# Attention inside a decoder layer: groups of score products and of value products kept whole in TensorE's order

## The chip, the cores and the metric

The kernel runs on one core of one Trainium2 chip. The metric is the device time of one execution in microseconds; the median of several runs is given. TensorE (PE in the profile, its weight loads PEld) multiplies matrices into PSUM banks; VectorE (DVE), ScalarE (ACT) and GpSimd (POOL) do the element-wise work; SyncE (SP) issues most DMAs.

## The reference

One decoder layer in float32: 2048 tokens, model width 1024. An RMS norm and one input projection give queries, keys and values for an attention with a window of 128 tokens, and the input of a convolution branch; both branches go through one output projection; a SwiGLU network with inner width 2816 follows.

```python
q = proj[..., :512].reshape(B, S, 8, 64)            # 8 query heads
k, v = ...                                          # 2 key/value heads of 64, 4 query heads share one
# blocks of 128 queries; each sees its own block of keys and the one before
s = jnp.einsum("bnqhgd,bnkhd->bnhgqk", qb, kb) * scale
s = jnp.where(in_band & not_before_start, s + bias, -inf)
m = jnp.maximum(max(s), sink)
p = jnp.exp(s - m); p = p / (sum(p) + jnp.exp(sink - m))
o = jnp.einsum("bnhgqk,bnkhd->bnqhgd", p, vb)
conv_out = conformer_conv(u, ...)                   # GLU, causal depthwise conv of width 31, LayerNorm, silu, pointwise
h = h + rms_norm(concat([o, conv_out]) @ w_out, mix_post_g)
h = h + rms_norm((silu(hn @ w_gate) * (hn @ w_up)) @ w_down, ffn_post_g)
```

## The kernel before

The tokens are worked on in four tiles of 512 (t = 0 to 3). Stage A_t makes the input projection of tile t, one output block of 128 columns after the other (`proj(u)`: 24 products of 128x128 by 128x512, since each float32 operand is split in a high and a low half and three products are made of each pair). Stage B_t is the attention of tile t, C_t the convolution branch with its 31 taps on VectorE, U a folding of weights, W_w the output projection, H and F the first half of the feed-forward network, G its second half. The names stand behind the @ in the tiles of the profile (`tr@B`, `mm@A`).

**Generators and lanes.** Each stage is a Python generator that emits instructions and then yields an estimate of TensorE's time. `run` drives the main stages; after each yield it pumps the lanes (`lb` for attention, `lc` for taps, `lw`, `ld`, `lf`, `lh` and others) by that estimate. So attention instructions are emitted between the projections of the next tile: B0 beside A1, B1 beside A2, and so on. Each instruction gets a running number as priority (`tc.cur_priority`; a smaller number goes first; the taps' lane adds 100). At build time a scheduler puts the instructions of each engine in a fixed order, by these numbers and by its own timeline of when operands and buffers will be there. On the chip each engine works its list in that order and waits at semaphores.

**Ties.** `tc.add_manual_dep` with the class `NoSync` only says that one instruction comes after another in the scheduler's order; with `Sync` the instruction also waits on a semaphore for the other to finish.

**Attention of a block of 128 queries.** `front(b)` makes the scores. Head pairs are stacked so that the two key/value heads lie in the two halves of the partitions; a product uses 64 of the 128 rows of the array, and the products of the two halves (g = 1 and 0) go to two PSUM banks. For each `ip` (0 and 1) two query tiles are used: twelve products into two banks, one group. TensorE's `tr` banks are three, shared by scores, transposes and value products. VectorE then masks (`copy_predicated`, L451) and adds the bias while taking the maximum (`tensor_tensor_reduce`, L454). `back(b)` normalizes, transposes the probabilities on TensorE (L491), ACT copies them (L492), POOL cuts them to the window's two triangles (`affine_select`, L494), and the value products follow: four products of 128 rows by 64 columns of the array, into the two halves of one bank, each in float32 and seen as two records in the profile (the first block has half of them). The order of emission is front(0), front(1), back(0), front(2), back(1), front(3), back(2), back(3).

`after_first(first, r)` ties a product behind another with `NoSync`. In a score group all products are tied behind the second, the second behind the first; in a value group all are tied behind the first. Nothing ties a group to another, and nothing holds the first product until the rest can go: in a group the first product is of g = 1, and the second, of g = 0, writes to the other bank.

All products go through the helper `mat` (L85), so in the profile they share that line and are told apart by their tiles: `tr@B<-kz,ql@A` are scores, `tr@B<-p@B,vtok` value products, `mm@...` products that use the whole array.

Of the kernel before, what the change touches and what calls it, by code (L numbers as in the profile page):

```python
# [12 lines left out]
F32 = mybir.dt.float32  # L13
# [5 lines left out]
ALU = mybir.AluOpType  # L19
# [18 lines left out]
def layer_kernel(ctx, tc, x, xT, cols, rows, sinks, relb, onehot, w_in, w_pw, w_out, w_gate, w_up, w_down, out):  # L38
# [22 lines left out]
    def f2(tag, shape=(P, T)):  # L61
        return t_(tag, shape)
# [108 lines left out]
            stt(y, w, d, y, ALU.add, ALU.mult)  # L171
        return y

    def after_first(first, r):
        tc.add_manual_dep(
            r.ins,
            first.ins.name,
            mybir.DependencyInfo(mybir.DependencyClass.NoSync, mybir.DependencyReason.DATA),
            reason="both halves of the array start together",
        )  # L180

    def three(o, pairs, first=True, last=True):
# [59 lines left out]
    y_scr = dr.tile([4, P, S], F32, name="y_scr")  # L242
    hT = [dr.tile([KC, P, T], F32, name=f"hT{i}") for i in range(2)]
    qs = {}
    started = set()

    def load_x(t):
# [74 lines left out]
    def stage_a(t, hn, before_kv, hooks, post=None):  # L322
        L = f"A{t}"
        lab[0] = L
        raw0 = [w0 if t == 0 else None]
        rb = None

        def proj(u):
            w = kweight(u, t > 0, raw0.pop() if raw0 else None)
            o = mm()  # L330
            for k in range(KC):
                three(o, [(w[k], (hn[k][:, 0], hn[k][:, 1]))], k == 0, k == KC - 1)
                for _ in range(FILL[k] if t == u == 0 else 0):
                    mat(warm[:, 0:P], ident, ident, start=True, stop=True)
            return o

        def step(u):
            if u in hooks:
                hooks[u]()
            lab[0] = L  # L340

        def glu(c, og, oa):
            lab[0] = L
            th = f2("fa")
            if post:
                vtt(th, og, rb, ALU.mult)
                act(th, th, AF.Tanh, scale=0.5)
            else:
                act(th, og, AF.Tanh, scale=0.5)
            if oa is None:  # L350
                oa = yield th
            g = f2("fa")
            stt(g, th, 1.0, oa, ALU.add, ALU.mult)
            if post:
                (ptt if 2 * c < TAPS0 else vtt)(g, g, rb, ALU.mult)
            nc.sync.dma_start(glu_scr[c, :, t * T : (t + 1) * T], g)
            started.add(f"g{t}{c}")
            yield

        for c in range(4):  # L360
            og = proj(2 * c)
            if post and c == 0:
                yield 5.2
                step(0)
                late = og, proj(1)
                next(post)
                yield 5.2
                step(1)
                continue
            if post and c == 1:  # L370
                rb = next(post)
                next(glu(0, *late))
            half = glu(c, og, None)
            next(half)
            yield 5.2
            step(2 * c)
            half.send(proj(2 * c + 1))
            yield 5.2
            step(2 * c + 1)
        before_kv()  # L380
        lab[0] = L
        ok = proj(8)
        if t:
            act(kz[:, :, 0:P], kz[:, :, T : T + P].bitcast(F32), AF.Copy)
        if post:
            kt = f2("fa")
            vtt(kt, ok, rb, ALU.mult)
            ok = kt
        act(kz[:, 0, P:], ok, AF.Copy)
        vtt(kz[:, 1, P:], ok, kz[:, 0, P:].bitcast(F32), ALU.subtract)  # L390
        yield 5.2
        step(8)
        ov = proj(9)
        vt = f2("fa")
        if post:
            vtt(vt, ov, rb, ALU.mult)
        else:
            act(vt, ov, AF.Copy)
        yield 5.2
        step(9)  # L400
        q = []
        for i in range(4):
            oq = proj(10 + i)
            if i == 0:
                pv = mm()
                for s in range(4):
                    nc.tensor.transpose(pv[:, s * P : (s + 1) * P], vt[:, s * P : (s + 1) * P], ident)
                if t:
                    nc.vector.tensor_copy(vtok[:, 0], vtok[:, 4])
                nc.vector.tensor_copy(vtok[:, 1:5].rearrange("p a b -> p (a b)"), pv)  # L410
            qi = hl("ql")
            if post:
                qt = f2("fa")
                stt(qt, oq, 0.125, rb, ALU.mult, ALU.mult)
                act(qi[:, 0], qt, AF.Copy)
                vtt(qi[:, 1], qt, qi[:, 0].bitcast(F32), ALU.subtract)
            else:
                act(qi[:, 0], oq, AF.Copy, scale=0.125)
                stt(qi[:, 1], oq, 0.125, qi[:, 0].bitcast(F32), ALU.mult, ALU.subtract)
            q.append(qi)  # L420
            yield 5.2
            step(10 + i)
        qs[t] = q

    def stage_b(t):
# [3 lines left out]
        def front(b):  # L429
            lab[0] = L  # L430
            first = t == 0 and b == 0
            tok = slice(b * P, (b + 1) * P)
            win = slice(b * P, b * P + 256)
            mx = sm(8)
            pr = f4("p", (P, 8, P))
            for ip in range(2):
                os = [tr().rearrange("p (j k) -> p j k", j=2) for _ in range(2)]
                lead = []
                for j in range(2):
                    i = 2 * ip + j  # L440
                    for n, (a, k) in enumerate(((0, 0), (0, 1), (1, 0))):
                        for g in (1, 0):
                            sl = slice(64 * g, 64 * g + 64)
                            r = mat(os[g][:, j], q[i][sl, a, tok], kz[sl, k, win], start=n == 0, stop=n == 2)
                            if lead:
                                after_first(lead[-1], r)
                            if len(lead) < 2:
                                lead.append(r)
                for g in range(2):
                    prev = neg.unsqueeze(2).to_broadcast([P, 2, P]) if first else os[g][:, :, 0:P]  # L450
                    nc.vector.copy_predicated(os[g][:, :, P:], upper.unsqueeze(1).to_broadcast([P, 2, P]), prev)  # L451
                    for j in range(2):
                        h = 4 * g + 2 * ip + j
                        nc.vector.tensor_tensor_reduce(  # L454
                            out=pr[:, h],
                            in0=os[g][:, j, P:],
                            in1=bias[0][:, h],
                            op0=ALU.add,
                            op1=ALU.max,
                            scale=1.0,  # L460
                            scalar=NEG,
                            accum_out=mx[:, h : h + 1],
                        )
                yield 1.3
                lab[0] = L
            negm = sm(8)
            stt(negm, mx, -1.0, nsnk, ALU.mult, ALU.min)
            es = sm(8)
            vtt(es, negm, snk, ALU.add)
            act(es, es, AF.Exp)  # L470
            den = sm(8)
            for h in range(8):
                act(pr[:, h], pr[:, h], AF.Exp, bias=negm[:, h : h + 1], accum_out=den[:, h : h + 1])
            vtt(den, den, es, ALU.add)
            rd = sm(8)
            nc.vector.reciprocal(rd, den)
            live[b] = pr, rd
            yield YC

        def back(b):  # L480
# [3 lines left out]
            for g in range(2):  # L484
# [6 lines left out]
                    nc.tensor.transpose(o[:, i * P : (i + 1) * P], pr[:, 4 * g + i], ident)  # L491
                act(pg[:, 1], o, AF.Copy)  # L492
                for kb in range(1 if first else 0, 2):
                    nc.gpsimd.affine_select(  # L494
                        out=pg[:, kb].rearrange("p (i q) -> p i q", q=P),
                        in_=pg[:, 1].rearrange("p (i q) -> p i q", q=P),
                        compare_op=ALU.is_ge if kb else ALU.is_gt,
                        fill=0.0,
                        base=0,
                        pattern=[[0, 4], [1 if kb else -1, P]],  # L500
                        channel_multiplier=-1 if kb else 1,
                    )
# [3 lines left out]
            lab[0] = L  # L506
            o = tr()
            lead = None
            for kb in (1,) if first else (1, 0):
                for g in (1, 0):  # L510
                    sl = slice(64 * g, 64 * g + 64)
                    r = mat(o[sl], vtok[:, b + kb, sl], pt[g][:, kb], start=kb == 1, stop=first or kb == 0)
                    if lead is None:
                        lead = r
                    else:
                        after_first(lead, r)
            at = f2("at")
            act(at, o, AF.Copy)
            c0 = t * T + b * P
# [3 lines left out]
            yield 1.8  # L523

        live = {}
        for b in range(5):
            if b < 4:
                yield from front(b)
# [820 lines left out]
    RT = 0.2  # L1349
    RP = 0.1  # L1350
    TIE = 5
    AHEAD = 3
    PRES = {0: 20, 2: 16}
    Q0 = 8
# [171 lines left out]
```

## Time and profile before

| what | value |
|---|---|
| median of 3 runs | 1982.09 us (1979.29 to 1984.77) |
| profiled execution | 1987.9 us, its span 1986.2 us |
| mean granted clock of TensorE | 0.987 |
| attention's products on TensorE | 98 to 586 us of the span |
| score products | 384, of 64x256 |
| value records | 124, of 128x512 |

The span runs from the first to the last instruction of the profiled execution; the time is some 1.7 us longer. In the timeline each row gives the start in us, the duration, the engine, the line, the operation, output<-inputs, the shape and a count of like instructions in a row; in brackets stands idle time before it and what ended it. Matmuls are pipelined, so that rows overlap: what one costs is seen from its start to the start of the next. In the table of stretches, PEclk is the granted share of TensorE's clock and DMA the mean busy share of the 16 DMA engines. "issue" as the end of a wait means that the engine waited for nothing that the profile shows.

### The profile page before, as it was taken

What the parts mean: (1) busy time and instruction counts of PE and PEld (TensorE: products, weight loads), DVE (VectorE), ACT (ScalarE), POOL (GpSimd) and SP (SyncE); (2) the same over time, 40 slices, a digit from 0 to 9 for tenths busy, and PEclk for the clock granted to TensorE, in tenths of its full rate; (3) what the DMA queues carried; (4) which work ended last, traced back from release to release, by engine and by line L of the source; (5) the groups of instructions that cost most, each with busy time, mean ns of one, the idle gap of its engine ahead of it and who ended that gap; (6) DMA issues with size and microseconds to landing.
All of it is one profiled execution on the core that took longest, in us unless ns stands there. A gap on an engine that the chain in (4) does not pass through costs nothing.

```text
span 1986.2 us, 26652 instructions
## 1 busy us (share of the span) xinstructions
PE 1930.4 (97%) x8730; PEld 1546.7 (78%) x8730; DVE 1476.3 (74%) x2648; ACT 961.8 (48%) x1886; POOL 304.3 (15%) x427
## 2 busy tenths in 40 slices
PE   8999999999999699999999999999899999999997
PEld 6877777777777588778888878887688888888886
DVE  5999969995874899787759965666866775555557
ACT  5455354447647544334345464656533433345443
POOL 4011011111121101220000110000023332311003
PEclk9999999999999799999999999999899999999999
DMA  8787657566658668775478777759844542375664
GB/s 311 251 303 219 210 187 256 185 212 214 225 195 281 232 218 266 260 266 184 130 253 276 259 255 242 249 202 309 293 140 169 179 140 96 132 244 181 211 195 144
DMA packets 209578, 435.67 MB, mean 219 GB/s; under 512 B 21752, under 2 KB 39328, under 8 KB 209440
## 3 DMA queue, kind: packets, MB, share of 16 engines
q1 hardware_dynamic: 191648, 402.52, 60.7%
q0 software_dynamic: 7040, 23.07, 3.5%
q10 hardware_dynamic: 10752, 8.39, 1.3%
q8 instruction: 68, 1.11, 0.2%
q14 instruction: 70, 0.57, 0.1%
HBM read 323.26 MB, written 110.63 MB: 218 GB/s over the span
## 4 chain that ended last, share of the span: by engine, by line
PE 77%; DVE 8%; DMA 7%; issue 3%; POOL 2%; ACT 2%; SPq 0%; DVEq 0%; POOLq 0%; ACTq 0%
PE mm@F L85 32%; PE mm@G L85 16%; PE mm@A L85 15%; PE mm@W L85 4%; PE tr@B L85 4%; PE tr@W L85 2%; DVE fc@C L94 2%; DMA wx@G<-w_down 1%; DMA gb@F<-keeps 1%; PE mm@U L85 1%; DVE w@F L94 1%; DVE hl@G L94 1%; PE tr@B L491 1%; DMA td<-wx@G 1%; DMA fc@G<-w_down 1%
## 5 line engine op out<-in xcount | busy, mean ns | idle before, releaser
L94 DVE SCALAR_TENSOR_TENSOR fc@C<-glu@C,colt,fc@C 128x512 f32<-128x512 f32 x480 | 357.3, 758 | 2.6
L85 PE MATMUL mm@F<-hl@H,w@F 128*128 128x512 f32 x1056 | 261.3, 397 | 10.2 <-ACT mm@F L939 10.2
L85 PEld LDWEIGHTS mm@F<-hl@H,w@F 128*128 128x128 f32 x1056 | 201.0, 192 | 54.6 <-ACT mm@F L939 12.5
L85 PE MATMUL mm@G<-hl@G,hl@G 128*128 128x512 f32 x924 | 227.7, 393 | 1.1 <-DVE hl@G L94 1.1
L821 ACT ACTIVATE w@F<-chl@F 128x512 fp32r<-128x512 f32 x220 | 135.9, 626 | 187.8 <-PE mm@F L85 149.6
L85 PE MATMUL mm@A<-hl@A,w@A 128*128 128x512 f32 x840 | 209.5, 397 | 4.2 <-ACT w@A L127 1.5
L85 PEld LDWEIGHTS mm@G<-hl@G,hl@G 128*128 128x128 f32 x924 | 171.7, 188 | 37.3 <-DVE hl@G L94 1.9
L85 PE MATMUL mm@G<-w@G,hl@G 128*128 128x512 f32 x876 | 199.4, 389 | 0.0
L85 PEld LDWEIGHTS mm@G<-w@G,hl@G 128*128 128x128 f32 x876 | 164.4, 188 | 34.1
L85 PEld LDWEIGHTS mm@A<-hl@A,w@A 128*128 128x128 f32 x840 | 156.6, 189 | 42.9 <-issue 3.3
L94 DVE TENSOR_TENSOR w@F<-chl@F,w@F 128x512 fp32r<-128x512 f32 x198 | 151.4, 768 | 49.0 <-ACT w@F L821 48.8
L85 PE MATMUL mm@F<-mid@H,w@F 128*128 128x512 f32 x528 | 136.5, 398 | 20.3 <-ACT w@F L821 13.3
L85 PEld LDWEIGHTS mm@F<-mid@H,w@F 128*128 128x128 f32 x528 | 101.0, 192 | 43.7 <-ACT w@F L821 14.1
L85 PE MATMUL mm@F<-ql@H,w@F 128*128 128x512 f32 x528 | 130.0, 392 | 0.0
L85 PE MATMUL mm@F<-p@H,w@F 128*128 128x512 f32 x528 | 129.1, 389 | 0.0
L85 PE MATMUL mm@F<-x@H,w@F 128*128 128x512 f32 x528 | 126.9, 391 | 0.0
L85 PEld LDWEIGHTS mm@F<-ql@H,w@F 128*128 128x128 f32 x528 | 99.1, 189 | 20.8
L85 PEld LDWEIGHTS mm@F<-p@H,w@F 128*128 128x128 f32 x528 | 99.1, 188 | 20.6
L85 PEld LDWEIGHTS mm@F<-x@H,w@F 128*128 128x128 f32 x528 | 98.4, 188 | 21.1 <-issue 0.8
L127 ACT ACTIVATE w@A<-raw@A 128x512 fp32r<-128x512 f32 x110 | 67.5, 626 | 92.1 <-PE mm@A L85 62.1
L94 DVE TENSOR_TENSOR w@G<-raw@G,w@G 128x512 fp32r<-128x512 f32 x73 | 52.1, 713 | 73.0 <-ACT w@G L821 71.8
L494 POOL TENSOR_SCALAR_AFFINE_SELECT p@B<-p@B 128x512 f32<-128x512 f32 x62 | 51.7, 843 | 338.4 <-ACT p@B L492 337.1
(314 smaller groups left out, 3290.1 us busy)
## 6 DMA issues: line engine op xcount, KB each, us to landing
mids<-fa@F SPq DMA_DIRECT2D x154, 256.0 KB, 2.7
raw@A<-w_in SPq DMA_DIRECT2D x55, 512.0 KB, 4.6
w@A<-lo_in SPq DMA_DIRECT2D x84, 256.0 KB, 3.3
fc@G<-mids SPq DMA_DIRECT2D x77, 256.0 KB, 3.4
fa@G<-mids SPq DMA_DIRECT2D x75, 256.0 KB, 4.4
gb@F<-keeps SPq DMA_DIRECT2D x72, 256.0 KB, 3.5
w@W<-fold SPq DMA_DIRECT2D x32, 512.0 KB, 5.9
raw@F<-w_gate SPq DMA_DIRECT2D x22, 512.0 KB, 4.0
```

The costliest lines, as they stand in the source:

```text
L85: r = nc.tensor.matmul(*args, **kw)
L94: r = op(*args, **kw)
L127: act(w[:, 0], raw, AF.Copy)
L491: nc.tensor.transpose(o[:, i * P : (i + 1) * P], pr[:, 4 * g + i], ident)
L494: nc.gpsimd.affine_select(out=pg[:, kb].rearrange("p (i q) -> p i q", q=P), in_=pg[:, 1].rearrange("p (i q) -> p i q", q=P), compare_op=AL ...
L821: act(w[:, 0], x, AF.Copy)
```

## The change

`after_first` gets an argument for the kind of tie. Three things follow in stage B. First, groups get an order among each other: the first product of a score group is tied (order only) behind the last product of the group before it, the first value product behind the last score product, and the next score group behind the last value product (`group[0]`). Second, the first product waits on semaphores: a score group's for the second reduction (g = 0, j = 1) of the score group before it (`scored[0]`), in block 0 also for the low half of its second query tile (`q_ready`); a value group's for the last `affine_select` (`cut`). Third, the products of both kinds are emitted with a priority number that is smaller by 100 (`SOON`).

```diff
-    def after_first(first, r):
+    def after_first(first, r, how="NoSync"):
         tc.add_manual_dep(
             r.ins,
             first.ins.name,
-            mybir.DependencyInfo(mybir.DependencyClass.NoSync, mybir.DependencyReason.DATA),
-            reason="both halves of the array start together",
+            mybir.DependencyInfo(getattr(mybir.DependencyClass, how), mybir.DependencyReason.DATA),
+            reason="products of half the array stand together",
         )
...
+    q_ready = {}
...
-                vtt(qi[:, 1], qt, qi[:, 0].bitcast(F32), ALU.subtract)
+                r = vtt(qi[:, 1], qt, qi[:, 0].bitcast(F32), ALU.subtract)
             else:
                 act(qi[:, 0], oq, AF.Copy, scale=0.125)
-                stt(qi[:, 1], oq, 0.125, qi[:, 0].bitcast(F32), ALU.mult, ALU.subtract)
+                r = stt(qi[:, 1], oq, 0.125, qi[:, 0].bitcast(F32), ALU.mult, ALU.subtract)
             q.append(qi)
+            q_ready.setdefault(t, []).append(r)
...
                 lead = []
+                before = group[0]
+                p0 = tc.cur_priority
+                tc.cur_priority = p0 - SOON
                 for j in range(2):
...
                             if lead:
                                 after_first(lead[-1], r)
+                            else:
+                                for e, how in ((before, "NoSync"), (scored[0], "Sync"), (None if b else q_ready[t][2 * ip + 1], "Sync")):
+                                    if e is not None:
+                                        after_first(e, r, how)
                             if len(lead) < 2:
                                 lead.append(r)
+                            group[0] = r
+                tc.cur_priority = p0
...
-                        nc.vector.tensor_tensor_reduce(
+                        e = nc.vector.tensor_tensor_reduce(
...
+                        if g == 0 and j == 1:
+                            scored[0] = e
...
-                    nc.gpsimd.affine_select(
+                    cut = nc.gpsimd.affine_select(
...
             lead = None
+            p0 = tc.cur_priority
+            tc.cur_priority = p0 - SOON
             for kb in (1,) if first else (1, 0):
                 for g in (1, 0):
                     sl = slice(64 * g, 64 * g + 64)
                     r = mat(o[sl], vtok[:, b + kb, sl], pt[g][:, kb], start=kb == 1, stop=first or kb == 0)
                     if lead is None:
                         lead = r
+                        after_first(group[0], r)
+                        after_first(cut, r, "Sync")
                     else:
                         after_first(lead, r)
+            group[0] = r
+            tc.cur_priority = p0
...
         live = {}
+        group, scored = [None], [None]
...
+    SOON = 100
```

## The prediction

> **What bounds the kernel now.** I read the page's busy times and chain first, then the table of stretches over the part of the span in which the attention runs, then the waits there, and last TensorE's timeline.
>
> ```profile
> span 1986.2 us, 26652 instructions
> PE 1930.4 (97%) x8730; PEld 1546.7 (78%) x8730; DVE 1476.3 (74%) x2648; ACT 961.8 (48%) x1886; POOL 304.3 (15%) x427
> PE 77%; DVE 8%; DMA 7%; issue 3%; POOL 2%; ACT 2%; SPq 0%; DVEq 0%; POOLq 0%; ACTq 0%
> ```
>
> ```profile
> core 0: us, PE busy (x) PEld busy (x) DVE busy (x) ACT busy (x) POOL busy (x), PEclk, DMA share, GB/s
> 98.00:216.00 118.00, 118.00 (x585) 90.20 (x585) 111.95 (x250) 65.58 (x165) 15.47 (x26) 1.00 0.78 259
> 216.00:340.00 124.00, 124.00 (x605) 90.85 (x602) 105.20 (x244) 62.83 (x155) 17.37 (x28) 1.00 0.66 212
> 340.00:478.00 138.00, 138.00 (x660) 104.32 (x659) 115.83 (x258) 67.34 (x166) 21.51 (x55) 1.00 0.67 216
> 478.00:590.00 112.00, 112.00 (x547) 81.44 (x546) 88.64 (x205) 64.90 (x158) 18.84 (x28) 1.00 0.57 196
> ```
>
> TensorE (PE) carries the chain that ends last, and from 98 to 590 us, where all products of the stages B0 to B3 lie, it is never idle: 492 of 492 us, at the full granted clock. VectorE (DVE) comes second: 112 of 118 us in the first stretch, 80 to 85% in the rest. A stage in which PE is never idle gets shorter only if PE needs less time for the same products. So the question is what PE loses inside its busy time.
>
> ```profile
> PEld tr@B L85 <- issue: 38.1, 94, 0.8
> PEld tr@B L85 <- DVE fc@C L94: 2.2, 4, 0.8
> ```
>
> These are the waits of the weight loads in 98:590. Ahead of those of the attention's products stand 38.1 us in 94 gaps which no other engine ended ("issue"); only a few short ones were ended by another engine. The timeline shows what the gaps are. First the plain price of a projection's product and a group of twelve score products that stands whole:
>
> ```profile
> 351.24 3.79 PE L85 MATMUL mm@W<-w@W,hl@W 128*128 128x512 f32 x16
> 354.95 0.97 PE L85 MATMUL tr@B<-kz,ql@A 64*128 64x256 f32 x12
> 355.86 1.66 PE L85 MATMUL mm@W<-w@W,hl@W 128*128 128x512 f32 x6
> 357.36 0.60 PE L549 MATMUL ct@C<-ident,fc@C 128*128 128x128 f32 x4
> ...
> 394.64 2.88 PE L85 MATMUL mm@A<-mid@A,w@A 128*128 128x512 f32 x12
> 397.36 2.88 PE L85 MATMUL mm@A<-hl@A,w@A 128*128 128x512 f32 x12
> ```
>
> I count from start to start, since the ends are modelled. Twelve full products take 397.36 - 394.64 = 2.72 us, 0.227 each. The whole score group takes 355.86 - 354.95 = 0.91. The sixteen full products before it take 3.71 instead of 16 x 0.227 = 3.63, the six behind it 1.50 instead of 1.36. So entering the half-array products costs 0.08 us and leaving them 0.14, 0.22 for the pair. Now a group whose first product stands alone:
>
> ```profile
> 221.53 0.38 PE L85 MATMUL tr@B<-kz,ql@A 64*128 64x256 f32 x1
> 221.84 4.61 PE L85 MATMUL mm@A<-hl@A,w@A 128*128 128x512 f32 x19
> 226.38 0.97 PE L85 MATMUL tr@B<-kz,ql@A 64*128 64x256 f32 x12
> ```
>
> The lone product takes 0.31 us, and the nineteen products behind it 4.54 instead of 4.31, another 0.23 for leaving and entering again. That is 0.54 us for a product which inside its group costs some 0.08. Last, value products that stand whole with a score group behind them, and value products between which score products have slipped:
>
> ```profile
> 170.86 1.94 PE L85 MATMUL tr@B<-p@B,vtok 128*64 128x512 f32 x8
> 172.73 0.97 PE L85 MATMUL tr@B<-kz,ql@A 64*128 64x256 f32 x12
> 173.63 1.69 PE L85 MATMUL mm@A<-chl@A,w@A 128*128 128x512 f32 x6
> ...
> 374.47 1.07 PE L85 MATMUL tr@B<-p@B,vtok 128*64 128x512 f32 x2
> 375.47 0.38 PE L85 MATMUL tr@B<-kz,ql@A 64*128 64x256 f32 x1
> 375.78 1.07 PE L85 MATMUL tr@B<-p@B,vtok 128*64 128x512 f32 x2
> ...
> 380.08 3.06 PE L85 MATMUL mm@A<-mid@A,w@A 128*128 128x512 f32 x12
> ```
>
> The eight value records and twelve score products take 2.77 us when they stand apart (1.87 and 0.90) and 380.08 - 374.47 = 5.61 us when they alternate. One such place costs 2.84 us.
>
> **The change, part by part.** No product, evacuation or transfer is added or removed, and no queue of SP, ACT or POOL gets or loses a DMA. What changes is TensorE's order, and the first product of each group waits for what its later members need.
>
> *Scores.* Merged as above, the timeline has 72 pieces of score products; the first and the last of them, and the last piece of value products, are
>
> ```profile
> 98.44 0.39 PE L85 MATMUL tr@B<-kz,ql@A 64*128 64x256 f32 x2
> ...
> 559.24 0.97 PE L85 MATMUL tr@B<-kz,ql@A 64*128 64x256 f32 x11
> ...
> 584.38 1.94 PE L85 MATMUL tr@B<-p@B,vtok 128*64 128x512 f32 x8
> ```
>
> From the start of each to the start of whatever comes next they take 39.7 us together. There are 32 groups (16 blocks, two each); whole they take 32 x 0.91 = 29.1. That removes 10.6 us.
>
> *Values.* There are 29 pieces with 38.6 us. The first block has half the records and takes 1.00 us (as 374.47 to 375.47), the other fifteen 1.87: 29.1 in all. That removes 9.5 us.
>
> *Entries and exits.* Of those 101 pieces 68 come behind full-array work. With whole groups there are 32 + 16 = 48, and eight score groups have their turn right behind a value group (as at 172.73), without full-array work between: 40. That removes 28 x 0.22 = 6.2 us, or 4.4 if those eight come apart.
>
> The gross saving is 10.6 + 9.5 + 6.2 = 26.3 us, all of it time in which PE is the bound.
>
> *The waits.* The first score product now waits for the reductions of the group before (they free a bank) and, in a stage's first block, for the second query tile; the value group's first product names the last mask of POOL, which it reads anyway. PE works in order, so behind such a head all projection products queue, and behind those their evacuations on ACT and DVE. In the old order the second product of a group waited for that same bank. How much room there is:
>
> ```profile
> 222.13 0.28 DVE L454 CUSTOM_DVE_ANT_0 p@B<-tr@B,mb@X 128x128 f32<-128x128 f32 x1
> ```
>
> ```profile
> 372.47 1.84 POOL L494 TENSOR_SCALAR_AFFINE_SELECT p@B<-p@B 128x512 f32<-128x512 f32 x2 [3.23 <-ACT p@B L492]
> ```
>
> The reduction ends at 222.41 and the group that needs its bank goes on at 226.38, 4.0 us later. The mask ends at 374.31 and the value product starts at 374.47, 0.16 us later. So heads have between nothing and 4 us to spare. As the price of a head I bound from below by zero (heads in the old order stand on the same releases, and the two DVE rows of waits sum to little) and from above by 0.55 us, the first of its 0.8 us gaps that DVE ended (2.2 us in 4). Averaged over 48 heads the old order pays 2.2 / 48 = 0.05; with more heads at the front of the queue I take 0.08, that is 4 us, because most release times don't move. The ends are 0 and 26 us.
>
> *Priority* moves the groups ahead of up to 100 steps of the program. It costs nothing on PE itself, the sum of products being the same; what it displaces are projection products, which have the whole stage as cover. If that cover is gone, it shows as the waits just priced.
>
> *Whether DVE lets the saving through.* By stretch, with the same count of pieces, PE saves about 4, 9, 5 and 8 us; DVE has 6, 19, 22 and 23 us free there. In the first it is nearly full, and I take off 2 us. The conv taps that fill it are all still to be done.
>
> *After 590 us* the order is the old one. One stall of PE stands there, 12.6 us behind DVE's sums:
>
> ```profile
> 685.10 1.22 PE L85 MATMUL mm@F<-mid@H,w@F 128*128 128x512 f32 x2 [12.61 <-ACT w@F L821]
> ```
>
> ```profile
> 680.00:690.00 10.00, 1.91 (x4) 1.09 (x5) 10.00 (x18) 4.11 (x7) 0.89 (x2) 0.50 0.54 196
> 690.00:700.00 10.00, 10.00 (x35) 7.99 (x34) 10.00 (x17) 4.01 (x7) 2.72 (x6) 0.75 0.84 286
> ```
>
> Those sums read what PE itself transposes among the products before, so the stall moves forward with PE and neither grows nor shrinks. What was late next, DVE's work there, is late again by the same amount.
>
> The sum: 26.3 - 4 - 2 = 20 us. The profiled execution took 1987.9 us (span 1986.2 and 1.7 around it), so it would become 1968; it lies 0.3% above the median of the runs, 1982.09, and for the median I say 1982 - 20 = 1962 us.
>
> **Rivals.**
>
> *DVE becomes the bound.* For it: 112 of 118 us busy in 98:216, and the taps are tied to products, so a faster PE asks for them sooner. Against: 15 to 20% free later. If nothing is saved in the first stretch (4 us) and half in the rest (11 of 22), with heads at 2 us more, the net is 26 - 4 - 11 - 2 = 9 to 10 us: 1972.
>
> *The groups don't stay whole.* An order tie says who comes after whom, not who may come between; if projection products still fit in between, as the chains at 374 us did, only the places where values and scores alternate go, or nothing does: 1982, between 1977 and 1986.
>
> *The heads stall (slower).* The place is the first product of each group. If priority moves it forward by one projection, 24 x 0.227 = 5.4 us, a room of 4.0 us turns into a wait of 1.4, and all projections queue behind it. The eight score groups behind a value group have their bank long since; the other 40 heads would wait 56 us in all, and 56 - 26 = 30 us are lost: 2012. It decides from 26.3 / 40 = 0.66 us for a head. For it: TensorE did nothing else in the 12.6 us before 685.10, though products with all inputs ready were queued. "TensorE: Matmul & The Clock Gate" of the Trainium skill (Part 2, step by step) says the same as a rule: only weight loads are pulled ahead, products stay in program order; by it each wait of a head is lost whole. Against: the waits of the old order total a few us.
>
> *The clock drops.* After the stall the granted clock is 0.50, and 0.75 in the ten us behind it. If five heads waited 4 us each, they would cost 5 x 4 and, at 0.75, about 2.5 us each after: 32 us, less the saving 26: 1988. The same page of the Trainium skill (HAM oscillation) puts the limit at about 3.4 us of idle time; the trace agrees that 12.6 us are enough, and no row here shows where the limit is.
>
> **How the numbers follow.** The forecast has a chance of 0.54, DVE as the bound 0.16, groups not whole 0.11, stalled heads 0.16, the clock 0.03. A measurement of this kernel tells about 0.3% (6 us) from no change. The forecast and DVE as the bound are faster, 0.70, and of the groups not whole 0.02 are; the rest of those, 0.08, is no change and 0.01 slower. So: faster 0.72, same 0.08, slower 0.20. The range begins at 1953, where heads cost nothing (26 us) and a rearranged order gives 3 more, and reaches up to 1988, which takes in DVE as the bound, the groups not whole, and the cheapest of the stalls; some 0.16 stay above, 0.04 below. The forecast's own range is 1954 to 1970.
>
> **What would show it.** Right: 32 pieces of scores of 0.9 us and 16 of values of 1.87 in the timeline; the "issue" gaps of tr@B's weight loads near 20 us instead of 38.1; PE's busy count in 98:590 complete at some 20 us earlier, and the stall near 672 us earlier by as much. DVE as the bound: PE idle before 250 us, ended by DVE. Stalled heads: PEld tr@B waiting for DVE p@B or POOL p@B, tens of us. The prediction is wrong if pieces with one or two products remain in number, or if those waits exceed the saving.

## The result, and the profile after

Before 1984.77 us (median of 7 runs, 1979.29 to 1989.89), after 1971.96 us (7 runs, 1969.59 to 1977.01): ratio 0.9941, 95% interval 0.9924 to 0.9958. The gain is 12.8 us by medians. The profiled execution of after took 1977.01 us, the longest of its seven, with a span 11.1 us shorter than that of before. First the page, busy times and chain, then the table of stretches over the same four stretches as before:

```profile
span 1975.1 us, 26656 instructions
PE 1910.5 (97%) x8730; PEld 1540.9 (78%) x8730; DVE 1474.2 (75%) x2648; ACT 961.0 (49%) x1886; POOL 303.0 (15%) x427
PE 70%; DVE 13%; DMA 10%; issue 3%; ACT 2%; POOL 1%; SPq 0%; DVEq 0%; POOLq 0%; ACTq 0%
```

```profile
core 0: us, PE busy (x) PEld busy (x) DVE busy (x) ACT busy (x) POOL busy (x), PEclk, DMA share, GB/s
98.00:216.00 118.00, 116.79 (x596) 90.42 (x596) 114.06 (x254) 65.99 (x166) 15.73 (x26) 1.00 0.79 265
216.00:340.00 124.00, 123.69 (x633) 95.08 (x632) 107.49 (x244) 64.57 (x159) 18.92 (x28) 1.00 0.67 219
340.00:478.00 138.00, 134.80 (x672) 103.49 (x670) 117.21 (x269) 73.41 (x171) 21.10 (x55) 1.00 0.67 218
478.00:590.00 112.00, 111.24 (x570) 85.63 (x569) 95.74 (x205) 65.58 (x165) 19.44 (x28) 1.00 0.60 211
```

TensorE is busy for 19.9 us less over the span, and the span is only 11.1 shorter: the rest is idle time that was not there before. In every stretch more products are done than before (596, 633, 672, 570 against 585, 605, 660, 547), and TensorE now waits: 1.2, 0.3, 3.2 and 0.8 us. The share of VectorE in the chain goes from 8 to 13%. The waits from 90 to 590 us, TensorE's rows and the first row of its weight loads:

```profile
PE mm@W L85 <- DVE x@W L94: 2.1, 1, 2.1
PE tr@B L85 <- DVE sm@A L94: 1.2, 1, 1.2
PE ct@H L836 <- ACT gb@H L837: 0.8, 1, 0.8
PE mm@A L85 <- DVE x@W L94: 0.7, 1, 0.7
...
PEld tr@B L85 <- issue: 28.5, 74, 1.6
```

One gap of 1.2 us stands ahead of a group of half-array products. The largest, 2.1 us, stands ahead of the output projection. The timeline shows the groups, and this wait:

```profile
375.12 1.94 PE L85 MATMUL tr@B<-p@B,vtok 128*64 128x512 f32 x8
...
376.99 0.97 PE L85 MATMUL tr@B<-kz,ql@A 64*128 64x256 f32 x12
...
377.90 4.62 PE L85 MATMUL mm@W<-w@W,hl@W 128*128 128x512 f32 x19
...
382.10 1.40 DVE L94 SCALAR_TENSOR_TENSOR fc@C<-glu@C,colt,fc@C 128x512 f32<-128x512 f32 x2
...
383.91 0.67 DVE L94 TENSOR_TENSOR x@W<-x@W,mm@W 128x512 f32<-128x512 f32 x1
...
384.64 1.65 PE L85 MATMUL mm@W<-w@W,hl@W 128*128 128x512 f32 x6 [2.12 <-DVE x@W L94]
```

The place near 375 us, which took 5.61 us when values and scores alternated, takes 377.90 - 375.12 = 2.78. Then TensorE wants a bank of the output projection whose sum (`x@W`) stands on VectorE behind two taps of the convolution (`fc@C`) and the reductions of the scores, and waits 2.12 us.

To see where the time went I count both traces from the start of TensorE's product number 400 to that of number 2800, the same 2400 products, by what each takes to the start of the next, with idle time apart:

| us | before | after | difference |
|---|---|---|---|
| score products | 39.7 | 30.4 | -9.3 |
| value products | 38.6 | 29.0 | -9.6 |
| all others | 416.1 | 412.9 | -3.3 |
| TensorE idle | 0 | 5.5 | +5.5 |
| these 2400 products | 494.4 | 477.8 | -16.6 |

Product 400 itself starts 1.4 us later than before, and from number 2800 to the end 4.2 us are given back: +1.6 up to number 3200 and +2.8 from 3450 to 4000, with little change after. These counts compare one execution of each kernel, and the times of one kernel spread by 7 to 11 us here; so what lies outside the stretch may belong in part to the execution and not to the change. In the first of the two places lies the stall. Its rows in the timeline, and VectorE in it by stretch; then the same stretch of before:

```profile
672.38 1.22 PE L85 MATMUL mm@F<-mid@H,w@F 128*128 128x512 f32 x2 [13.98 <-ACT w@F L841]
...
676.65 1.22 PE L85 MATMUL mm@F<-ql@H,w@F 128*128 128x512 f32 x2 [3.05 <-ACT w@F L841]
```

```profile
658.30:672.40 14.10, 0.12 (x2) 0.03 (x1) 14.10 (x24) 4.86 (x9) 3.77 (x7) 0.68 0.60 206
```

```profile
672.40:685.10 12.70, 0.09 (x2) 0.01 (x1) 12.70 (x22) 4.41 (x8) 2.15 (x4) 0.59 0.59 211
```

VectorE is busy throughout both times; 24 of its operations now lie in the stall, 22 before, and it lasts 13.98 us instead of 12.61. In the second place (3450 to 4000) idle time is the same, 6.0 us, and the products themselves take 2.7 us more; the granted clock there is 0.97 and 0.95 in two stretches (806 to 836 and 836 to 881 us) where it was 0.94 and 1.00 (820 to 850 and 850 to 892). By these shares 0.03 x 30 + 0.05 x 45 = 3.15 us of clock are missing after the change, and 0.06 x 30 = 1.8 before: some 1.4 of the 2.7 us, an estimate. The rest stays open.

### The profile page after: what moved, and what is told of

Read it like the earlier page. It is cut to its first block, busy times and chain, and to the rows that moved or that the text cites. A ratio compares the mean times of both kernels' runs of the same rounds, so it can differ in the third digit from the quotient of the medians.

```text
span 1975.1 us, 26656 instructions
## 1 busy us (share of the span) xinstructions
PE 1910.5 (97%) x8730; PEld 1540.9 (78%) x8730; DVE 1474.2 (75%) x2648; ACT 961.0 (49%) x1886; POOL 303.0 (15%) x427
## 4 chain that ended last, share of the span: by engine, by line
PE 70%; DVE 13%; DMA 10%; issue 3%; ACT 2%; POOL 1%; SPq 0%; DVEq 0%; POOLq 0%; ACTq 0%
PE mm@F L85 33%; PE mm@G L85 16%; PE mm@A L85 10%; DVE fc@C L94 4%; PE mm@W L85 3%; PE tr@W L85 2%; PE tr@B L85 2%; DMA mids<-fa@F 1%; DMA gb@F<-keeps 1%; DMA raw@F<-w_up 1%; DVE hl@G L94 1%; PE mm@U L85 1%; DMA raw@F<-w_gate 1%; PE tr@B L504 1%; PE ct@H L836 1%
## 5 line engine op out<-in xcount | busy, mean ns | idle before, releaser
L507 POOL TENSOR_SCALAR_AFFINE_SELECT p@B<-p@B 128x512 f32<-128x512 f32 x62 | 55.9, 908 | 337.7 <-ACT p@B L505 336.2
```

What stands on the lines that cost most here:

```text
L507: cut = nc.gpsimd.affine_select(out=pg[:, kb].rearrange("p (i q) -> p i q", q=P), in_=pg[:, 1].rearrange("p (i q) -> p i q", q=P), compare ...
```

## The experiments

The table has all kernels. A piece is a run of products of one kind with no other between them, an entry a place where half-array work follows other work; both are counted in TensorE's order. The columns in us are those of the count above. In e1, e3, e7 and e11 up to eight records of half-array products fall outside the count, and as many others inside, so that single columns are off by up to 2 us there and the sum is not. In e2 and in e5 to e12 some products behind a wait ran at half the granted clock (the last section has an example), so that their columns hold a little of that too. Each ratio is to before in the same round of runs, with medians of 1984.77 (after), 1985.10 (e1 to e4), 1985.62 (e5 to e8) and 1983.07 us (e9 to e12). By times alone e1, e3, e4, e8, e10, e11 and e12 can't be told from the change, since their intervals overlap with its; e2, e5, e6, e7 and e9 lie clear of it.

| kernel | pieces S / V / entries | scores | values | others | idle | sum | median, us | ratio to before, 95% |
|---|---|---|---|---|---|---|---|---|
| before | 72 / 29 / 68 | 39.7 | 38.6 | 416.1 | 0 | 494.4 | 1984.77 | |
| after | 37 / 16 / 43 | 30.4 | 29.0 | 412.9 | 5.5 | 477.8 | 1971.96 | 0.9941 (0.9924, 0.9958) |
| e1 no waits | 59 / 16 / 65 | 34.8 | 29.0 | 417.1 | 1.4 | 482.2 | 1977.35 | 0.9957 (0.9941, 0.9974) |
| e2 no priority | 38 / 22 / 52 | 30.7 | 32.5 | 415.9 | 7.1 | 486.1 | 1982.83 | 0.9992 (0.9978, 1.0006) |
| e3 values only | 63 / 16 / 73 | 37.3 | 27.2 | 419.0 | 0 | 483.5 | 1978.77 | 0.9961 (0.9950, 0.9973) |
| e4 scores only | 37 / 24 / 44 | 30.2 | 37.0 | 411.6 | 1.7 | 480.5 | 1977.49 | 0.9958 (0.9943, 0.9973) |
| e5 before, more VectorE work | 73 / 29 / 67 | 40.5 | 41.9 | 418.8 | 10.2 | 511.3 | 2003.16 | 1.0081 (1.0061, 1.0101) |
| e6 after, more VectorE work | 36 / 16 / 42 | 30.6 | 30.8 | 415.4 | 18.0 | 494.7 | 1989.32 | 1.0010 (0.9995, 1.0025) |
| e7 normalizing on GpSimd | 36 / 16 / 42 | 29.9 | 27.2 | 416.5 | 9.5 | 483.0 | 1985.37 | 0.9992 (0.9979, 1.0005) |
| e8 sums of w_down on GpSimd | 35 / 16 / 41 | 30.5 | 29.0 | 413.5 | 4.6 | 477.6 | 1981.15 | 0.9966 (0.9950, 0.9981) |
| e9 no group order | 44 / 27 / 42 | 31.9 | 36.6 | 414.6 | 7.0 | 490.0 | 1986.02 | 1.0011 (0.9995, 1.0026) |
| e10 taps later | 34 / 16 / 40 | 30.2 | 30.8 | 412.7 | 10.6 | 484.2 | 1976.53 | 0.9960 (0.9945, 0.9975) |
| e11 priority 50 | 32 / 18 / 42 | 29.2 | 29.2 | 413.9 | 6.8 | 479.1 | 1975.52 | 0.9957 (0.9940, 0.9974) |
| e12 priority 200 | 34 / 16 / 40 | 30.3 | 29.0 | 413.5 | 6.4 | 479.2 | 1974.47 | 0.9947 (0.9928, 0.9966) |

**The parts of the change.** First without the waits:

```diff
-   for e, how in ((before, "NoSync"), (scored[0], "Sync"), (None if b else q_ready[t][2 * ip + 1], "Sync")):
+   for e, how in ((before, "NoSync"),):
...
-                        after_first(cut, r, "Sync")
```

> The change without the semaphore waits of the first products: order ties and priority stay. Its fixed order has 59 pieces of scores, 16 of values and 65 entries from full-array work (before: 72, 29, 68; after: 37, 16, 43). Theory (price by the piece): scores 36.1 us, values 29.0, entries 0.22 each, gross 13.8 us less TensorE time than before against 24.4 with the whole change; some of it is given back by VectorE, so 1974 to 1981 us, slower than the whole change. Rival (heads that wait hold TensorE, and that is where 20 predicted became 13): without waits TensorE is idle less and the kernel is at 1972 or faster.

The values are whole, of the scores only 15 groups. The lone first products are back, as at 222 us:

```profile
222.38 0.38 PE L85 MATMUL tr@B<-kz,ql@A 64*128 64x256 f32 x1
222.69 4.61 PE L85 MATMUL mm@A<-hl@A,w@A 128*128 128x512 f32 x19
227.22 0.97 PE L85 MATMUL tr@B<-kz,ql@A 64*128 64x256 f32 x12
```

TensorE waits 4.1 us less than after the change, and its products take 8.6 us more. So the waits of the first products cost about four us and buy twice that, since the scheduler, which is told of them, then leaves a group until all of it can go. Next without priority:

```diff
-    SOON = 100
+    SOON = 0
```

> The change with SOON = 0: ties and waits stay. Order: 38 pieces of scores, 22 of values, 52 entries. Theory: scores 30.5 us, values 32.4, gross 18.9 us less than before; VectorE is full in the same places but is asked for later, so idle time of TensorE in the attention 2 to 6 us; 1970 to 1978 us. Rival (priority brings the groups forward so that their heads and the evacuations behind them come late): idle time under 2 us and the time at or below the whole change's 1972.

By medians the gain is gone, and neither forecast time came out. Six more pieces of values cost 3.4 us, others 3.0, idle time 1.6; that is 8.3 of the 16.6 us in this stretch. Its waits from 90 to 590 us stand at the attention itself, most of them:

```profile
PE tr@B L85 <- DVE sm@B L465: 2.7, 2, 1.5
PE tr@B L504 <- DVE p@B L94: 2.5, 2, 1.6
PE mm@A L85 <- DVE x@W L94: 1.3, 1, 1.3
PE tr@B L85 <- POOL p@B L507: 0.3, 1, 0.3
PE mm@W L85 <- DVE fa@A L94: 0.3, 1, 0.3
```

Its times lie in two groups, 1977.7 to 1980.9 and 1984.7 to 1987.4, and the profiled execution (1979.36) is of the first; where the second loses the rest no trace shows. Then each half alone: in e3 the ties, wait and priority of the value groups, and none of those of the scores; in e4 the reverse.

```diff
-                tc.cur_priority = p0 - SOON
...
-   for e, how in ((before, "NoSync"), (scored[0], "Sync"), (None if b else q_ready[t][2 * ip + 1], "Sync")):
+   for e, how in ():
```

> Only the value groups get the tie, the wait and the priority; scores as before. Order: 63 pieces of scores, 16 of values, 73 entries. Theory: scores 37.2 us, values 29.0, entries 1 us more than before, gross 11.0 us less; 1975 to 1981 us. If scores and values add up, this and the scores-only kernel have 27 us gross between them against 24 for the whole change. Rival (the saving is from the scores): 1982 or more.

```diff
-            tc.cur_priority = p0 - SOON
...
-                        after_first(group[0], r)
-                        after_first(cut, r, "Sync")
...
-            group[0] = r
```

> Only the score groups get ties, waits and priority; values as before. Order: 37 pieces of scores, 24 of values, 44 entries. Theory: scores 30.2 us, values 37.0, gross 16.4 us less than before; 1971 to 1979 us. Rival (the saving is from the values): 1980 or more.

In the stretch the halves save 11.0 and 13.9 us. Their products alone save 11.0 and 15.6, together 26.6, and those of the whole change 22.1; idle times are 0, 1.7 and 5.5. By medians each half brings two thirds of the gain. The two halves together lack 8.3 us of their sum (11.0 + 13.9 against 16.6). By the pieces 4.5 of these are savings that either half makes: both take away places where scores and values alternate (e3 has nine pieces of scores fewer than before, e4 five of values). The other 3.8 us are waits that neither half has alone. Last the order between groups left out, with waits and priority kept:

```diff
-   for e, how in ((before, "NoSync"), (scored[0], "Sync"), (None if b else q_ready[t][2 * ip + 1], "Sync")):
+   for e, how in ((scored[0], "Sync"), (None if b else q_ready[t][2 * ip + 1], "Sync")):
...
-                        after_first(group[0], r)
```

> The waits of the first products and the priority, without the order ties between groups. The order now has 44 pieces of scores (28 whole), 27 of values and 42 entries. Theory (the saving is the sum of the prices of the pieces, less the time TensorE waits): scores -10 us, values -1 us, entries -5 us, some -15 in the stretch of the attention, and with the 3 to 6 us that are lost behind it 1974 to 1977. Rival (the order between groups is what matters, since without it a value group and a score group mix): values stay at 38 us and the gain is under 5 us, 1980.

The rival held, and more: the values stay at 36.6 us, no time is gained. The 4.4 us that the stretch is shorter than before are given back behind it (3.8 in the profiled execution). Values and scores still alternate, as at 257 us:

```profile
257.52 1.07 PE L85 MATMUL tr@B<-p@B,vtok 128*64 128x512 f32 x2
258.53 0.38 PE L85 MATMUL tr@B<-kz,ql@A 64*128 64x256 f32 x1
258.84 1.07 PE L85 MATMUL tr@B<-p@B,vtok 128*64 128x512 f32 x2
259.84 0.38 PE L85 MATMUL tr@B<-kz,ql@A 64*128 64x256 f32 x1
```

The order ties between groups, on which TensorE never waits, end this; 28 of the score groups are whole without them too.

**Does VectorE let the saving through?** Thirty-two extra operations of some 0.66 us on VectorE in the taps of the first two tiles (each adds zero times its input), in both kernels:

```diff
                 stt(y, g[:, j : j + T], dwh[:, c, j : j + 1], y, ALU.mult, ALU.add)
+                if t < 2 and j % 7 == 3:
+                    stt(y, g[:, j : j + T], 0.0, y, ALU.mult, ALU.add)
```

> The kernel before with 32 more taps of weight zero (4 for each channel block of tiles 0 and 1), about 21 us more work on VectorE beside the attention; the output stays the same. Theory (before the change TensorE alone bounds the attention, VectorE has 70 us to spare there): TensorE's time in the attention grows by 0 to 4 us, the kernel is at 1983 to 1990 us. Rival (VectorE bounds both kernels alike): 8 us or more, as much as on the changed kernel.

> The same 32 taps of weight zero on the changed kernel. Theory (what the change saves on TensorE is let through only as far as VectorE keeps up, and VectorE is now the bound in parts of the attention): idle time of TensorE in the attention grows from 5.5 us by 5 to 15 us and the kernel loses 5 to 15 us, 1977 to 1987, clearly more than the kernel before loses. Rival (the 5.5 us are an accident of the order and VectorE has room): loss under 4 us.

Some 21 us of work on VectorE cost 17.5 us by medians before the change (2003.16 against 1985.62), and 17.4 after it (1989.32 against 1971.96, of two rounds; by the ratios the prices are some 16 and 14 us). In the count both stretches grow by 16.9 us. In e5 10.2 of these are idle time and 6.7 are slower products, with a clock of 0.94 in the last stretch. That the kernel before would swallow it, with TensorE never idle there, was wrong. Between the loaded kernels the change still saves 13.8 us. Were VectorE the bound only after the change, the load would cost more there. The table of stretches of e5, and the first waits of e6 from 90 to 590 us:

```profile
340.00:478.00 138.00, 138.00 (x661) 104.37 (x660) 130.49 (x272) 61.71 (x155) 24.06 (x41) 1.00 0.68 211
478.00:590.00 112.00, 103.89 (x469) 70.18 (x470) 80.70 (x200) 61.60 (x149) 17.03 (x31) 0.94 0.45 154
```

```profile
PE ct@C L633 <- ACT yt@C L638: 6.1, 2, 4.3
PE ct@H L838 <- ACT gb@H L839: 2.6, 2, 1.8
```

The price is paid where the taps are due, not where VectorE is fullest: the end of the convolution branch (`ct@C`) comes late, and from 478 us on TensorE waits (8.1 us in e5, 11.2 in e6) while VectorE is busy 72% of the stretch in e5.

**Can the new waits be taken away by relieving VectorE?** In e7 the 32 normalizing multiplications of the attention go to GpSimd, in e8 the subtractions of the folding of `w_down`; in e10 the taps get a priority lag of 400 in place of 100.

```diff
-                vtt(pr[:, hs], pr[:, hs], rd[:, hs].unsqueeze(2).to_broadcast([P, 4, P]), ALU.mult)
+                ptt(pr[:, hs], pr[:, hs], rd[:, hs].unsqueeze(2).to_broadcast([P, 4, P]), ALU.mult)
```

> The changed kernel with the 32 multiplications that normalize the probabilities on GpSimd instead of VectorE: 21 us less work for VectorE in the attention. Its order has 36 pieces of scores and 16 of values, as the changed kernel. Theory (VectorE gives back part of the saving): idle time of TensorE in the attention falls from 5.5 us to 0 to 2, and the kernel gains 2 to 6 us: 1966 to 1970. Rival (GpSimd takes longer for it and the value products' heads wait): idle time under tr@B grows, 1972 or more.

```diff
-                vtt(o, p_, q_, ALU.subtract)
+                ptt(o, p_, q_, ALU.subtract)
```

> The changed kernel with the 44 subtractions of the stage between 590 and 720 us (the sums of w_down) on GpSimd instead of VectorE: 30 us less for VectorE around the stall of TensorE that the change lengthened from 15.6 to 17.0 us. Theory (that stall is VectorE's queue, in which the sums for the next products stand behind others): the stall falls to 8 to 13 us, the kernel gains 4 to 9 us, 1963 to 1968. Rival (the chain of sums itself sets the stall): the stall stays within 2 us of 17, 1970 to 1974.

```diff
-    RC0, RC1, RC2, RC3, RW0, RW, RB, LC = 0.7, 1.1, 0.4, 0.9, 1.7, 1.25, 0.8, 100
+    RC0, RC1, RC2, RC3, RW0, RW, RB, LC = 0.7, 1.1, 0.4, 0.9, 1.7, 1.25, 0.8, 400
```

> The change, and the lane of the convolution's taps 400 steps behind the others in priority instead of 100 (LC). The order has 34 pieces of scores, 16 of values, 40 entries. Theory (what TensorE still waits for in the attention's stretch, 5.5 us, is VectorE's sums and maskings queued behind taps): with the taps later TensorE's idle time there falls under 2 us, the stretch is 4 to 6 us shorter than after the change, the time 1966 to 1969. Rival (the taps have a due time of their own): the end of the convolution branch comes late, TensorE is idle between 478 and 590 us for 5 us or more, and the time is 1975 to 1985.

All three miss the theory's times. But e7 and e8 did not do what they were made for: VectorE was hardly relieved. The busy times of e7 and then of e8, to be held against 1474.2 us of VectorE in 2648 operations after the change:

```profile
PE 1908.3 (96%) x8730; PEld 1539.2 (78%) x8730; DVE 1472.5 (74%) x2616; ACT 961.0 (49%) x1886; POOL 349.1 (18%) x459
PE 1908.9 (96%) x8730; PEld 1538.8 (78%) x8730; DVE 1487.9 (75%) x2604; ACT 960.0 (49%) x1886; POOL 370.6 (19%) x471
```

With 32 operations fewer VectorE is busy for 1.7 us less, and with 44 fewer for 13.7 us more. Its other operations take longer while GpSimd works on the moved ones. In e7, of the 284 taps within the count, the 215 with no GpSimd operation beside them take 0.74 us in the mean, and the 21 beside a moved multiplication 1.14. An operation of another kind in e7, beside the second of two such multiplications, takes 1.53 us; four like it after the change, from 264 to 285 us, take 0.68 to 0.85:

```profile
280.37 3.01 POOL L500 TENSOR_TENSOR p@B<-p@B,sm@B 128x512 f32<-128x512 f32 x2 [3.93 <-ACT chl@U L127]
...
282.40 1.53 DVE L94 SCALAR_TENSOR_TENSOR yt@C<-fc@C,yt@C 128x512 f32<-128x512 f32 x1
```

Within the count VectorE is busy for 414.3 us in e7 and 421.1 after the change, 6.8 less where some 20 were meant to go. From product 2800 to 4000, where most of the sums of e8 lie, it is 258.4 us in e8 and 247.3 after the change. So these two kernels leave open what a VectorE with less to do would be worth.

In e7 idle time of TensorE grows from 5.5 to 9.5 us; in e8 it is 4.6, but the stall behind grows from 13.98 to 17.42 us, with 27 operations of VectorE in it (with the gap that follows, which the expectation counts in, from 17.0 to 19.9); in e10, which moves no work, idle time grows to 10.6 us. By medians e7 lies 13.4 and e8 9.2 us above the change; the profiled executions show 5.4 and 4.1 of it, in e7 within the stretch and in e8 behind it. The waits of e7 and then of e10 from 90 to 590 us, and the stall of e8:

```profile
PE mm@A L85 <- DVE x@W L94: 3.5, 1, 3.5
PE mm@A L85 <- DVE ql@A L94: 3.1, 1, 3.1
```

```profile
PE tr@B L85 <- POOL p@B L507: 2.1, 1, 2.1
PE mm@A L85 <- DVE ql@A L94: 1.7, 1, 1.7
PE ct@H L836 <- ACT yt@C L636: 1.7, 1, 1.7
PE mm@W L85 <- DVE x@W L94: 1.6, 1, 1.6
```

```profile
675.49 1.22 PE L85 MATMUL mm@F<-mid@H,w@F 128*128 128x512 f32 x2 [17.42 <-ACT w@F L841]
```

The waits for `x@W` are 3.5 us in e7 and 2.8 after the change (2.1 and 0.7), and one of 3.1 us for `ql@A` is new. The reading that fits is that the operations ahead of the awaited one in VectorE's fixed list decide, with how long each takes, and that each edit makes another list; this is argued and not shown. The stall goes with its count (22, 24 and 27 operations for 12.6, 14.0 and 17.4 us), while for e7 the list was not taken apart. In e10 TensorE waits for 3.6 us before 216 us and 3.8 from 478 on; the latter is the rival's place (the due time of the convolution), at a smaller size, and the time of 1976.53 us lies in the rival's range. Two more priorities:

```diff
-    SOON = 100
+    SOON = 50
```

> The change with a priority of 50 in place of 100. The order has 32 pieces of scores, all whole, 18 of values, 42 entries: by the prices of the pieces 0.7 us less than after the change. Theory: TensorE's idle time is about that of the change (5 us, and 7 without priority), so the time is within 2 us of the change's, 1970 to 1974. Rival (the priority decides what VectorE is asked for and when, so each value gives another queue there): idle time or the stall behind 670 us differ by 5 us or more, in either direction.

```diff
-    SOON = 100
+    SOON = 200
```

> The change with a priority of 200 in place of 100. The order has 34 pieces of scores, 16 of values, 40 entries: by the prices of the pieces 1.7 us less than after the change. Theory: groups with a higher priority push the taps back and TensorE waits no longer than after the change, 1968 to 1973. Rival (each value gives another queue on VectorE, and its waits come by chance): idle time or the stall behind 670 us differ by 5 us or more, in either direction.

By their pieces they should be 0.7 and 1.7 us better; both wait a little more (6.8 and 6.4 us), and both times lie 1.5 us above what the theory gave. Their intervals overlap with that of the change: between 50 and 200 the number matters little, and its being there at all matters (e2). In e11 the scores are as whole as they can be (32 pieces, 29.2 us), and the time isn't shorter for it. None of the versions beats the change measurably.

## Why the prediction was right, and where not

The median after lies 10 us above the forecast (1971.96 against 1962, with a median of before of 1984.77 against 1982.09), inside the range, and it is faster as the likeliest case said, but it misses that case's own range (1954 to 1970) by 2 us: 12.8 us were gained and not 20. The groups became whole and the products cheaper as told; what went wrong is what becomes of the saving. By the steps:

- **Scores and values**: -9.3 and -9.6 us measured, -10.6 and -9.5 in the sum. The prices held. That the groups become whole held for 28 of 32 score groups (37 pieces instead of 32) and for all 16 of values. For values it is the order between groups that does it (e9: 27 pieces without it); for scores it is more the waits (e1: 15 whole groups without them, e9: 28 without the order).
- **Entries and exits**: mis-sized. The sum had 6.2; measured are -3.3 for all other products. There are 43 entries, not 40. The products next to half-array work save 4.6 by the count, and plain ones and those beside transposes take 1.2 more, which the sum didn't have.
- **Waits of the heads and VectorE's limit**: 4 + 2 us in the sum, 5.5 measured, but in other places, so that the size agrees by luck. One gap of 1.2 us is at a head; most of the rest is at products of the projections behind VectorE's sums. The step that held them to heads was incomplete: a bank of a projection is awaited as well when TensorE comes earlier.
- **Priority**, put at nothing: it costs nothing as predicted, but carries about half of the saving in the stretch (e2), which the prediction did not see.
- **"After 590 us" the stall neither grows nor shrinks**: this step failed. 4.2 us were given back behind product 2800, 1.4 of it in the first gap of the stall, where two more of VectorE's operations lie; the second place has no more idle time, only slower products. Orders differ in this without a rule that I found: 0.1 us is given back in e2, 1.3 in e11, 2.3 in e10, 3.8 in e3 and e9 and 8.3 in e8, and e6 gains 2.8; each is one execution. Together with 1.4 us at the start, which no experiment explains, it is most of the 9 us that the span's saving lacks to the 20 forecast.
- **The rivals**: "DVE becomes the bound" gave 1972, the very figure measured, so the time alone can't tell it from the forecast; but it came there by another way: nothing saved before 216 us and half lost after it. In the count the products' saving comes through nearly whole (22.1 gross, 5.5 waited), and e5 and e6 show the load on VectorE costing both kernels alike. What this rival had right is whom TensorE now waits for. But the free time of VectorE that I set against it (6, 19, 22 and 23 us) wasn't slack: the kernel before pays for extra work there as well. "Groups not whole" is what e9 is, with 1986 at its upper end. "Heads stall" needed 0.66 us for a head; 5.5 us over 48 heads would be 0.11 even if all stood there. "The clock drops" isn't seen: 1.00 in all four stretches, with no wait there above 2.1 us. That was not safe: in e8 nearly the same order and a wait of 2.14 us at the same place were followed by half the clock (last section).
- **The signs named**: of values as told; of scores 28 pieces of 0.9 us, not 32; the weight loads' "issue" gaps fell to 28.5, not 20 us; the stall begins 14.1 us earlier (658.4 instead of 672.5), not 20.

## What to carry to other kernels

An engine that is busy without a gap can still lose time inside its busy time: count from start to start, and look for short products of another shape strewn among full ones. An order tie between groups adds no wait on the chip, and a wait put on a group's first product lets the scheduler keep the group whole; here each of them, and a priority that brings the group forward as one, added to the saving. Expect some of it to be lost again in waits for the next engine, and don't take the idle share of an engine whose work has due times for slack. When work is moved from one engine to another, read the first one's busy time afterwards: here VectorE's hardly fell in e7, and rose in e8.

## What the runs showed of the hardware

Two value products that write to different halves of a bank run beside each other. In e9 a piece with one such product (two records) stands at 257.52 us, above; the same trace has pieces with four of them (eight records) and with two:

```profile
377.89 1.94 PE L85 MATMUL tr@B<-p@B,vtok 128*64 128x512 f32 x8
379.76 0.73 PE L85 MATMUL mm@W<-w@W,hl@W 128*128 128x512 f32 x2
...
454.41 1.08 PE L85 MATMUL tr@B<-p@B,vtok 128*64 128x512 f32 x4
455.42 0.33 PE L630 MATMUL ct@C<-ident,yt@C 128*128 128x128 f32 x1
```

One takes 258.53 - 257.52 = 1.01 us, two take 1.01, four 1.87. So a value group that is torn into four single products takes four times 1.0 us in place of 1.87, which is 2.1 of the 2.84 us that such a place costs. "TensorEngine Tiling (Array Packing)" of the Trainium skill (Key Properties) says that different tiles of the array work in parallel and that a change of the tiling mode drains the array; the trace agrees with the first, and the 0.22 us for entering and leaving half-array work are what a change costs here. That a drain is their cause no run shows.

The other surprise is the price of VectorE's work in a kernel whose TensorE had no idle time in that stretch: some 21 us more cost 17.5 us, of which 10.2 us are idle time that was not there before.

VectorE and GpSimd did not work independently of each other: the taps took 1.14 us in place of 0.74 beside the multiplications that e7 put on GpSimd. Why, no run here shows.

The granted clock, too, can fall at short waits. After the change TensorE waits 2.12 us at 384.64 us, and the clock stays at 1.00. In e8 the wait at this place is 2.14 us:

```profile
385.13 1.97 PE L85 MATMUL mm@W<-w@W,hl@W 128*128 128x512 f32 x6 [2.14 <-DVE x@W L94]
387.03 1.65 PE L85 MATMUL tr@B<-kz,ql@A 64*128 64x256 f32 x12
388.61 3.53 PE L85 MATMUL mm@A<-mid@A,w@A 128*128 128x512 f32 x12
```

```profile
386.40:389.70 3.30, 3.30 (x17) 2.25 (x16) 3.30 (x6) 0.00 (x0) 0.00 (x0) 0.50 0.21 83
```

The clock is 0.50 for these 3.3 us, and the group of scores takes 388.61 - 387.03 = 1.58 us instead of 0.91. What decides whether a wait of this length is followed by a lower clock, no run here shows.
